# The seven-product down projection: activation forms made in steps between products, and T4 by a negation on ScalarE and an accumulating DMA

## The chip, the core and the metric

The kernel runs on one core of a Trainium2 chip. The metric is the device time of one execution in microseconds. An engine is named by the profile's short names: PE (TensorE, matmuls), DVE (VectorE), ACT (ScalarE), POOL (GpSimd), SP (SyncE, which here only issues DMAs).

## What is computed

One layer of a decoder trunk on 256 tokens of width 2048, in float32. The mixers come first; the part that matters is the second half of the layer, with 8192 hidden columns:

```python
x = layer_norm(ALPHA * x + jnp.einsum('bse,ed->bsd', mixed, w_out[l]), ln1_g[l], ln1_b[l])
h = jnp.square(jax.nn.relu(jnp.einsum('bsd,df->bsf', x, w_up[l])))
x = layer_norm(ALPHA * x + jnp.einsum('bsf,fd->bsd', h, w_down[l]), ln2_g[l], ln2_b[l])
```

## The kernel before, in words

Every float32 operand of a matmul is split into a high part (a cast to fp32r on ACT, L90) and a low part (a subtraction on DVE, L91, `split_to`); a product is then three matmuls (hi hi, hi lo, lo hi). Weights are split in halves of 1024 columns into the tiles `hi` and `lo`, four buffers each, so the splits run up to four halves ahead of PE.

The hidden columns are cut into eight groups of 1024 (`FG`). While the down projection of group g runs, the up projection of group g+1 is made in eight units ("U": `up`, `unit_t`, 16 x 2 matmuls over one 1 MB load `raw`, then `act_up` with a copy on ACT, an addition on DVE and two activations on ACT). The activations of a group lie in `hs[g % 2]`.

The down projection of groups 0 to 6 runs by seven products in place of eight (Winograd's form of Strassen's scheme). Blocks of activations: A11, A12 (first 128 tokens), A21, A22 (last 128 tokens), each by the first and second 512 hidden columns of the group. Their forms are S1 = A21 + A22, S2 = S1 - A11, S3 = A11 - A21, S4 = A12 - S2. The eight forms, split, lie in `forms` (the tile `ms`). Weights come in blocks b11, b12, b21, b22 of 1 MB (`load_blocks`, one buffer each; b12 lies in `ry`); DVE makes from them T1 = b12 - b11 (L902), T2 = b22 - T1 (L905), T3 = T2 - b11 (L910), T4 = b21 - T2 (L913). A "pair" p is one half of the 2048 output columns: pair a is p = 0, pair b is p = 1. `pair_steps` yields between its products, which come in the order 1 (A11 b11), 2 (A12 b21), 3 (S4 b22), 6 (S2 T2), 5 (S1 T1), 7 (S3 T3), 4 (A22 T4). In the seventh group (g = 6) only pair a runs by seven products; its other half is made by `plain` ("c" and "d"), with A11 to A22 as they are.

Results of a product either stay in PSUM (`pk`; products 1, 5, 6, 7 of pair a) or are copied by ACT to a tile `new` (four buffers, shared with the sums of the forms) and added in SBUF by an accumulating DMA that POOL issues (L891), into `acc` (tile `rx`) or `macc` (tile `ry`). `pair_sums(1)`, in the last of these groups, and `pair_sums(0)`, after them, add the kept products up on DVE.

The order of the stage is written out by hand, a letter a step:

```python
TURNS = "UUaaaUaaaUaUbbbUbbbUbU"
LAST = "UUUaaaUaUaUaUaUcd"
...
if n == 0:
    make_blocks(g)
elif n == 1:
    make_sums(g)
elif n == 3 and g == FG - 2:
    pair_sums(1)
```

So splits of the blocks are written behind the first step of a group and the sums with their splits behind the second. From this text a scheduler of the framework fixes the order on each engine and each DMA queue ahead of the run: what it holds to be ready goes first, earlier text before later. Each engine then works strictly in its order. All loads of weights go through SP's queue.

Of the kernel before, what the change touches and what calls it, by code (L numbers as in the profile page):

```python
# [11 lines left out]
F32 = mybir.dt.float32  # L12
F32R = mybir.dt.float32r
AF = mybir.ActivationFunctionType
ALU = mybir.AluOpType
PSUM = bass.MemoryType.PSUM

P = 128
# [6 lines left out]
FG = 8  # L25
# [23 lines left out]
def trunk_kernel(ctx: ExitStack, tc: tile.TileContext, xT, x, w_qi, w_t, w_va, w_vm0, w_vm, w_vc,  # L49
                 w_oam, w_oc, w_up4, w_up, w_down, w_dnl, conv, bif, gm, gc, lamv, g1, b1, g2, b2, out):  # L50
    nc = tc.nc
# [37 lines left out]
    def split_to(src, hi, lo, eng=nc.vector):  # L89
        nc.scalar.copy(hi, src)  # L90
        eng.tensor_sub(lo, src, hi.bitcast(F32))  # L91
# [3 lines left out]
    def split(raw, a, b, eng=nc.vector):  # L95
        pool = wpools[turn[0] % len(wpools)]
        turn[0] += 1
        hi = pool.tile([P, 1024], F32R, tag="hi", name="hi", bufs=4)
        lo = pool.tile([P, 1024], F32R, tag="lo", name="lo", bufs=4)
        split_to(raw[:, a:b], hi[:, :b - a], lo[:, :b - a], eng)  # L100
        return hi, lo
# [121 lines left out]
    def mx(name):  # L223
        return psm.tile([P, 512], F32, tag="mx", name=name)
# [115 lines left out]
    def qk():  # L340
        return [tp.tile([P, S], F32, tag=n, name=n, bufs=2) for n in ("qh", "kh")]

    for h in range(HA):
        q, k = qk()
# [73 lines left out]
    for c in range(4):  # L418
        n = VM_N[c]
        src = [w_vm0[g] for g in range(4)] if c == 0 else [w_vm[c - 1, g] for g in range(4)]  # L420
# [93 lines left out]
    for h in range(HM):  # L514
        q, k = qk()
# [97 lines left out]
    for h in range(HC):  # L613
        q, k = qk()
# [7 lines left out]
    for c in range(4):  # L622
        pss = run_units([w_oam[c, g] for g in range(3)], 512, ms, range(12))
        for t in range(2):
            a = acc[:, t, 512 * c:512 * c + 512]
# [185 lines left out]
    def up(g, m):  # L811
        h = hs[g % 2]
        unit_t(w_up[FT * g + m - 4], lambda ps: act_up(ps, h, m))
# [7 lines left out]
    A11, A12, A21, A22, S1, S2, S3, S4 = range(8)  # L821
    HT = FT // 2
    forms = ms.rearrange("p a b -> p (a b)").rearrange("p (f s k t) -> p f s k t", f=8, s=2, k=HT)
# [5 lines left out]
    def blocks_of(h):  # L829
        return [[h[:, HT * k:HT * k + HT, P * t:P * t + P] for k in range(2)] for t in range(2)]  # L830

    def make_blocks(g):
        h = hs[g % 2]
        for t in range(2):
            src = h[:, :, P * t:P * t + P].rearrange("p (f k) t -> p f k t", f=2)
            split_to(src, forms[:, 2 * t:2 * t + 2, 0], forms[:, 2 * t:2 * t + 2, 1])

    def make_sums(g):
        a = blocks_of(hs[g % 2])

        def form(f, op, x, y):
            d = fp.tile([P, HT, P], F32, tag="new", name="sum", bufs=4)
            op(d, x, y)
            split_to(d, forms[:, f, 0], forms[:, f, 1])
            return d

        s1 = form(S1, nc.vector.tensor_add, a[1][0], a[1][1])
        s2 = form(S2, nc.vector.tensor_sub, s1, a[0][0])
        form(S3, nc.vector.tensor_sub, a[0][0], a[1][0])
        form(S4, nc.vector.tensor_sub, a[0][1], s2)  # L850

    def load_blocks(g, p):
        b11, b22, b21 = (fp.tile([P, 2048], F32, tag=n, name=n, bufs=1) for n in ("b11", "b22", "b21"))
        b12 = ry[:, 2048:4096]
        nc.sync.dma_start(b11, w_down[g, 2 * p, 0])
        nc.sync.dma_start(b12, w_down[g, 2 * p + 1, 0])
        nc.sync.dma_start(b22, w_down[g, 2 * p + 1, 1])
        nc.sync.dma_start(b21, w_down[g, 2 * p, 1])
        return b11, b12, b22, b21

    def product(g, p, i, f, b):

        if p == 0 and i in KEPT:
            if g == 0:
                kept[i] = mx("pk")
            ps, first, last = kept[i], g == 0, g == FG - 2
        else:
            ps, first, last = psb.tile([P, 512], F32, tag="big", name="pp"), True, True
        for q in range(2):
            hi, lo = split(b, 1024 * q, 1024 * q + 1024)  # L870
            for kk in range(2):
                k = 2 * q + kk
                w_hi, w_lo = hi[:, 512 * kk:512 * kk + 512], lo[:, 512 * kk:512 * kk + 512]
                nc.tensor.matmul(ps, forms[:, f, 0, k, :], w_hi, start=first and k == 0, stop=False)  # L874
                nc.tensor.matmul(ps, forms[:, f, 0, k, :], w_lo, start=False, stop=False)  # L875
                nc.tensor.matmul(ps, forms[:, f, 1, k, :], w_hi, start=False, stop=last and k == HT - 1)  # L876
        if p == 0 and i in KEPT:
            return
        if i in KEPT:
            a = macc[:, KEPT[i]]  # L880
            if g == 0:
                nc.scalar.copy(a, ps)
                return
        else:
            a = out_block(p, *((0, 0), (0, 1), (1, 0))[i - 2])
            if g == 0:
                nc.vector.scalar_tensor_tensor(a, a, ALPHA, ps, ALU.mult, ALU.add)
                return
        d = fp.tile([P, 512], F32, tag="new", name="new", bufs=4)
        nc.scalar.copy(d, ps)  # L890
        nc.gpsimd.dma_start(a, d, accum_op=ALU.add)  # L891

    def out_block(p, t, c):
        return acc[:, t, 1024 * p + 512 * c:1024 * p + 512 * c + 512]

    def pair_steps(g, p, blocks):

        b11, b12, b22, b21 = blocks
        product(g, p, 1, A11, b11)
        yield  # L900
        product(g, p, 2, A12, b21)
        nc.vector.tensor_sub(b12, b12, b11)  # L902
        yield
        product(g, p, 3, S4, b22)
        nc.vector.tensor_sub(b22, b22, b12)  # L905
        yield
        product(g, p, 6, S2, b22)
        yield
        product(g, p, 5, S1, b12)
        nc.vector.tensor_sub(b11, b22, b11)  # L910
        yield
        product(g, p, 7, S3, b11)
        nc.vector.tensor_sub(b21, b21, b22)  # L913
        yield
        product(g, p, 4, A22, b21)
        if p == 0 and g < FG - 2:
            pairs["b"] = pair_steps(g, 1, load_blocks(g, 1))
        yield
# [20 lines left out]
    def plain(g, c):  # L939

        pss = [psb.tile([P, 512], F32, tag="big", name="pst") for _ in range(2)]
        for i in range(2):
            raw = load_raw(w_down[g, c, i], 2048)
            for hf in range(2):
                hi, lo = split(raw, 1024 * hf, 1024 * hf + 1024)
                for kk in range(2):
                    k = 2 * hf + kk
                    w_hi, w_lo = hi[:, 512 * kk:512 * kk + 512], lo[:, 512 * kk:512 * kk + 512]
                    for t in range(2):
                        f = 2 * t + i  # L950
                        first, last = (i, k) == (0, 0), (i, k) == (1, HT - 1)
                        nc.tensor.matmul(pss[t], forms[:, f, 0, k, :], w_hi, start=first, stop=False)  # L952
                        nc.tensor.matmul(pss[t], forms[:, f, 0, k, :], w_lo, start=False, stop=False)  # L953
                        nc.tensor.matmul(pss[t], forms[:, f, 1, k, :], w_hi, start=False, stop=last)  # L954
        for t in range(2):
            a = acc[:, t, 512 * c:512 * c + 512]
            nc.vector.tensor_add(a, a, pss[t])
# [13 lines left out]
    fp = ctx.enter_context(tc.tile_pool(name="fp", bufs=1))  # L971
# [1 line left out]
    hs[1] = fp.tile([P, FT, S], F32, name="h1")  # L973


    TURNS = "UUaaaUaaaUaUbbbUbbbUbU"
    LAST = "UUUaaaUaUaUaUaUcd"
    for g in range(FG - 1):
        pairs = {"a": pair_steps(g, 0, load_blocks(g, 0))}
        units = iter(range(FT))  # L980
        for n, what in enumerate(TURNS if g < FG - 2 else LAST):
            if what == "U":
                up(g + 1, next(units))
            elif what in "cd":
                plain(g, "cd".index(what) + 2)
            else:
                next(pairs[what])
            if n == 0:
                make_blocks(g)
            elif n == 1:  # L990
                make_sums(g)
            elif n == 3 and g == FG - 2:
                pair_sums(1)
    pair_sums(0)

# [87 lines left out]
```

## Time and profile before

| | us |
|---|---|
| runs, median (lowest to highest) of 3 | 1206.28 (1202.72 to 1206.58) |
| the profiled execution | 1202.33 |
| its span | 1200.3 |
| PE busy in the span | 1151.7 |
| DVE busy | 939.6 |
| ACT busy | 699.8 |
| POOL busy | 65.7 |

The down-projection stage with its up-projection units lies at about 520 to 1130 us; groups 0 to 5 begin every 88 to 91 us. In the timelines of the profile an instruction's row gives its start, its duration and, in brackets, how long its engine had stood idle and what released it. Durations of neighbours on one engine overlap by some 0.1 us.

### The profile page before, as it was taken

How to read it: one execution, taken by the hardware profiler on the slowest of the kernel's cores; microseconds unless marked ns; L12 is line 12 of the kernel's file. 1: busy time of each engine (PE TensorE's matmuls, PEld its weight loads, DVE VectorE, ACT ScalarE, POOL GpSimd, SP SyncE). 2: the span in 40 equal slices, each digit the busy share in tenths (PEclk: the TensorE clock that was granted, in tenths of full speed). 3: DMA queues.
4: the chain of work that ended last, by engine and by line, in shares of the span. 5: the costliest groups of instructions: out<-in, count | busy, mean ns of one | idle time of the engine just before them, and what ended most of it. 6: DMA issues, size and time to landing. Idle time of an engine off the chain costs nothing. (4 is left out here: it accounts for less than half of the span.)

```text
span 1200.3 us, 15706 instructions
## 1 busy us (share of the span) xinstructions
PE 1151.7 (96%) x5960; PEld 981.9 (82%) x5960; DVE 939.6 (78%) x1225; ACT 699.8 (58%) x1010; POOL 65.7 (5%) x87
## 2 busy tenths in 40 slices
PE   9999999999999999989999999999989999989996
PEld 7998899988888887878787877878878878768885
DVE  5596556677667589598998898898898898878757
ACT  5444446545555453566676676676676676656641
POOL 1000000000000010000000100101101101100002
PEclk9999999999999999999999999999999999989998
DMA  8654446644854582545546847847837947844561
GB/s 303 217 186 165 144 159 235 212 172 175 300 187 147 179 305 100 185 166 220 210 158 229 273 147 236 278 136 237 289 123 236 293 119 237 264 166 132 175 246 70
DMA packets 42566, 240.41 MB, mean 200 GB/s; under 512 B 4982, under 2 KB 5372, under 8 KB 18556
## 3 DMA queue, kind: packets, MB, share of 16 engines
q1 hardware_dynamic: 33564, 218.19, 50.5%
q0 software_dynamic: 8208, 18.09, 7.7%
q10 hardware_dynamic: 720, 3.15, 0.7%
q8 instruction: 46, 0.75, 0.3%
q14 instruction: 28, 0.23, 0.1%
HBM read 223.41 MB, written 2.11 MB: 188 GB/s over the span
## 5 line engine op out<-in xcount | busy, mean ns | idle before, releaser
L158 PE MATMUL ps<-xs,hi 128*128 128x512 f32 x1488 | 526.4, 394 | 0.0
L90 ACT CAST hi<-raw 128x1024 fp32r<-128x1024 f32 (+4 forms) x307 | 310.5, 1015 | 288.0 <-PE ps L158 106.2
L91 DVE TENSOR_TENSOR lo<-raw,hi 128x1024 fp32r<-128x1024 f32 (+4 forms) x305 | 358.6, 1187 | 149.0 <-ACT hi L90 147.6
L159 PE MATMUL ps<-xs,lo 128*128 128x256 f32 x1488 | 421.8, 283 | 12.7 <-DVE lo L91 12.4
L158 PEld LDWEIGHTS ps<-xs,hi 128*128 128x128 f32 x1488 | 280.6, 189 | 58.7 <-issue 0.3
L159 PEld LDWEIGHTS ps<-xs,lo 128*128 128x128 f32 x1488 | 282.3, 190 | 19.6 <-DVE lo L91 18.3
L91 DVE TENSOR_TENSOR lo<-b,hi 128x1024 fp32r<-128x1024 f32 x156 | 185.6, 1221 | 32.1 <-ACT hi L90 32.1
L90 ACT CAST hi<-b 128x1024 fp32r<-128x1024 f32 x156 | 160.9, 1048 | 47.2 <-PE ps L158 15.9
L874 PE MATMUL pp<-hi,ms 128*128 128x512 f32 x252 | 101.4, 402 | 17.0 <-ACT hi L90 16.9
L875 PE MATMUL pp<-lo,ms 128*128 128x512 f32 x252 | 100.5, 399 | 0.4 <-DVE lo L91 0.3
L876 PE MATMUL pp<-hi,ms 128*128 128x512 f32 x252 | 100.3, 398 | 0.0
L208 PE MATMUL pst<-hi,xs 128*128 128x384 f32 (+3 forms) x224 | 79.0, 353 | 0.0
L209 PE MATMUL pst<-lo,xs 128*128 128x384 f32 (+3 forms) x224 | 77.7, 347 | 0.0
L210 PE MATMUL pst<-hi,xs 128*128 128x384 f32 (+3 forms) x224 | 77.6, 346 | 0.0
L874 PEld LDWEIGHTS pp<-hi,ms 128*128 128x128 f32 x252 | 47.7, 189 | 33.2 <-ACT hi L90 22.3
L875 PEld LDWEIGHTS pp<-lo,ms 128*128 128x128 f32 x252 | 47.6, 189 | 12.1 <-DVE lo L91 1.3
L876 PEld LDWEIGHTS pp<-hi,ms 128*128 128x128 f32 x252 | 47.8, 190 | 10.8
L891 POOL DMA_DIRECT2D rx<-new x33 | 28.1, 852 | 496.0 <-ACT new L890 441.0
L875 PE MATMUL pk<-lo,ms 128*128 128x512 f32 x112 | 44.4, 397 | 1.6 <-DVE lo L91 1.6
L874 PE MATMUL pk<-hi,ms 128*128 128x512 f32 x112 | 43.7, 398 | 1.5 <-ACT hi L90 1.5
L876 PE MATMUL pk<-hi,ms 128*128 128x512 f32 x112 | 44.4, 396 | 0.0
L890 ACT COPY new<-pp 128x512 f32<-128x512 f32 x53 | 30.9, 584 | 22.5 <-PE pp L876 22.5
(290 smaller groups left out, 1530.9 us busy)
## 6 DMA issues: line engine op xcount, KB each, us to landing
raw<-in_w_up_dram SPq DMA_DIRECT2D x64, 1024.0 KB, 7.2
b<-in_w_down_dram SPq DMA_DIRECT2D x39, 1024.0 KB, 6.8
raw<-in_w_t_dram SPq DMA_DIRECT2D x33, 1024.0 KB, 4.8
ry<-in_w_down_dram SPq DMA_DIRECT2D x13, 1024.0 KB, 5.1
raw<-in_w_oam_dram SPq DMA_DIRECT2D x12, 1024.0 KB, 4.9
raw<-in_w_vm_dram SPq DMA_DIRECT2D x12, 768.0 KB, 4.2
rx<-new POOLq DMA_DIRECT2D x33, 256.0 KB, 3.6
raw<-in_w_dnl_dram SPq DMA_DIRECT2D x8, 1024.0 KB, 7.1
```

Of the source, the lines that this page charges most:

```text
L90: nc.scalar.copy(hi, src)
L91: eng.tensor_sub(lo, src, hi.bitcast(F32))
L158: nc.tensor.matmul(ps, hi[:, P * kk:P * kk + P], xs[:, k, :], start=(k == 0), stop=False)
L159: nc.tensor.matmul(ps[:, 0:S], lo[:, P * kk:P * kk + P], xs[:, k, 0:S], start=False, stop=(k == KT - 1))
L208: nc.tensor.matmul(pss[t][:, :n], a_hi, w_hi, start=first, stop=False)
L209: nc.tensor.matmul(pss[t][:, :n], a_hi, w_lo, start=False, stop=False)
L210: nc.tensor.matmul(pss[t][:, :n], a_lo, w_hi, start=False, stop=last)
L874: nc.tensor.matmul(ps, forms[:, f, 0, k, :], w_hi, start=first and k == 0, stop=False)
L875: nc.tensor.matmul(ps, forms[:, f, 0, k, :], w_lo, start=False, stop=False)
L876: nc.tensor.matmul(ps, forms[:, f, 1, k, :], w_hi, start=False, stop=last and k == HT - 1)
L890: nc.scalar.copy(d, ps)
L891: nc.gpsimd.dma_start(a, d, accum_op=ALU.add)
```

## The change

- The forms come in steps. After the first step of a group the splits of A11 and A12 and the sums S1 and S2; after the second the sum S4 and the splits of S4 and S2; after the fourth the split of S1, S3 with its split, and A22 (in the seventh group A21 and A22). A21 is not split any more in the other groups, where no product reads it.
- T4 is not subtracted on DVE any more. After product 5 and T3, ACT multiplies b22 (which holds T2) by -1 in place, and a DMA issued by POOL adds b21 to it, read from DRAM a second time. Product 4 reads b22. So b21's tile is free after product 2, and b22's only after product 4.
- The turns change: in groups 0 to 5 "aaaUaaaUaU" becomes "aaaUaaUaUa" for either pair, in the seventh group a U moves ahead of product 7 and product 4 comes between "c" and "d". `pair_sums(1)` comes one step later.

```diff
--- before.py
+++ after.py
@@ -829,25 +829,25 @@
     def blocks_of(h):
         return [[h[:, HT * k:HT * k + HT, P * t:P * t + P] for k in range(2)] for t in range(2)]
 
-    def make_blocks(g):
+    def make_blocks(g, t):
         h = hs[g % 2]
-        for t in range(2):
-            src = h[:, :, P * t:P * t + P].rearrange("p (f k) t -> p f k t", f=2)
+        src = h[:, :, P * t:P * t + P].rearrange("p (f k) t -> p f k t", f=2)
+        if t == 0 or g == FG - 2:
             split_to(src, forms[:, 2 * t:2 * t + 2, 0], forms[:, 2 * t:2 * t + 2, 1])
-
-    def make_sums(g):
+        else:
+            split_to(src[:, 1], forms[:, A22, 0], forms[:, A22, 1])
+
+    sums = {}
+
+    def make_form(g, f):
         a = blocks_of(hs[g % 2])
-
-        def form(f, op, x, y):
-            d = fp.tile([P, HT, P], F32, tag="new", name="sum", bufs=4)
-            op(d, x, y)
-            split_to(d, forms[:, f, 0], forms[:, f, 1])
-            return d
-
-        s1 = form(S1, nc.vector.tensor_add, a[1][0], a[1][1])
-        s2 = form(S2, nc.vector.tensor_sub, s1, a[0][0])
-        form(S3, nc.vector.tensor_sub, a[0][0], a[1][0])
-        form(S4, nc.vector.tensor_sub, a[0][1], s2)
+        op, x, y = {S1: (nc.vector.tensor_add, a[1][0], a[1][1]), S2: (nc.vector.tensor_sub, sums.get(S1), a[0][0]),
+                    S3: (nc.vector.tensor_sub, a[0][0], a[1][0]), S4: (nc.vector.tensor_sub, a[0][1], sums.get(S2))}[f]
+        sums[f] = fp.tile([P, HT, P], F32, tag="new", name="sum", bufs=4)
+        op(sums[f], x, y)
+
+    def split_form(f):
+        split_to(sums[f], forms[:, f, 0], forms[:, f, 1])
 
     def load_blocks(g, p):
         b11, b22, b21 = (fp.tile([P, 2048], F32, tag=n, name=n, bufs=1) for n in ("b11", "b22", "b21"))
@@ -908,11 +908,13 @@
         yield
         product(g, p, 5, S1, b12)
         nc.vector.tensor_sub(b11, b22, b11)
+
+        nc.scalar.mul(b22, b22, -1.0)
+        nc.gpsimd.dma_start(b22, w_down[g, 2 * p, 1], accum_op=ALU.add)
         yield
         product(g, p, 7, S3, b11)
-        nc.vector.tensor_sub(b21, b21, b22)
         yield
-        product(g, p, 4, A22, b21)
+        product(g, p, 4, A22, b22)
         if p == 0 and g < FG - 2:
             pairs["b"] = pair_steps(g, 1, load_blocks(g, 1))
         yield
@@ -973,8 +975,8 @@
     hs[1] = fp.tile([P, FT, S], F32, name="h1")
 
 
-    TURNS = "UUaaaUaaaUaUbbbUbbbUbU"
-    LAST = "UUUaaaUaUaUaUaUcd"
+    TURNS = "UUaaaUaaUaUabbbUbbUbUb"
+    LAST = "UUUaaaUaUaUUaUcad"
     for g in range(FG - 1):
         pairs = {"a": pair_steps(g, 0, load_blocks(g, 0))}
         units = iter(range(FT))
@@ -986,10 +988,19 @@
             else:
                 next(pairs[what])
             if n == 0:
-                make_blocks(g)
+                make_blocks(g, 0)
+                make_form(g, S1)
+                make_form(g, S2)
             elif n == 1:
-                make_sums(g)
-            elif n == 3 and g == FG - 2:
+                make_form(g, S4)
+                split_form(S4)
+                split_form(S2)
+            elif n == 3:
+                split_form(S1)
+                make_form(g, S3)
+                split_form(S3)
+                make_blocks(g, 1)
+            if n == 4 and g == FG - 2:
                 pair_sums(1)
     pair_sums(0)
```

## Rows read from the trace of the kernel before

**Rows 1.** The page, part 1: busy us (share of the span) xinstructions, whole span

```profile
PE 1151.7 (96%) x5960; PEld 981.9 (82%) x5960; DVE 939.6 (78%) x1225; ACT 699.8 (58%) x1010; POOL 65.7 (5%) x87
```

**Rows 2.** Windows; columns PE, PEld, DVE, ACT, POOL, clock, DMA, GB/s

```profile
701.00:790.00 89.00, 84.62 (x426) 70.46 (x425) 78.34 (x71) 61.31 (x85) 8.51 (x10) 1.00 0.68 219
```

**Rows 3.** Timeline of PE: start us, us, engine, line, operation, [idle before <-releaser]

```profile
711.89 0.39 PE L158 MATMUL ps<-xs,hi 128*128 128x512 f32 x1
717.44 0.63 PE L874 MATMUL pk<-hi,ms 128*128 128x512 f32 x2
725.84 0.40 PE L158 MATMUL ps<-xs,hi 128*128 128x512 f32 x1
```

**Rows 4.** PE's waits (total us, times, longest): 520:612, 612:1040, 1040:1062

```profile
PE pk L875 <- DVE lo L91: 1.6, 1, 1.6
PE pk L874 <- ACT hi L90: 1.5, 1, 1.5
PE pp L874 <- ACT hi L90: 1.4, 1, 1.4
...
PE pp L874 <- ACT hi L90: 15.6, 10, 3.1
PE ps L159 <- DVE lo L91: 4.8, 8, 0.7
...
PE ps L159 <- DVE lo L91: 7.6, 2, 5.7
```

**Rows 5.** Timeline of PE, two waits of the group from 701 us

```profile
705.26 0.50 PE L874 MATMUL pp<-hi,ms 128*128 128x512 f32 x1 [2.24 <-ACT hi L90]
727.23 0.50 PE L874 MATMUL pp<-hi,ms 128*128 128x512 f32 x1 [0.98 <-ACT hi L90]
```

**Rows 6.** Windows of busy time, two stretches with a lowered clock

```profile
960.00:980.00 20.00, 17.86 (x83) 14.71 (x82) 18.25 (x22) 15.12 (x23) 0.55 (x1) 0.91 0.28 104
1060.00:1080.00 20.00, 18.86 (x86) 15.88 (x87) 19.53 (x23) 16.33 (x25) 0.56 (x1) 0.84 0.45 158
```

**Rows 7.** Groups by line, DVE, 701:790: xcount | busy us, mean ns | idle before

```profile
L91 DVE TENSOR_TENSOR lo<-b,hi 128x1024 fp32r<-128x1024 f32 x24 | 28.5, 1220 | 5.5 <-ACT hi L90 5.5
L913 DVE TENSOR_TENSOR b<-b,b 128x2048 f32<-128x2048 f32 x2 | 4.6, 2286 | 0.0
L843 DVE TENSOR_TENSOR sum<-h 128x512 f32<-128x512 f32 x3 | 2.1, 684 | 0.0
L91 DVE TENSOR_TENSOR ms<-sum,ms 128x512 fp32r<-128x512 f32 x4 | 2.6, 683 | 0.0
L91 DVE TENSOR_TENSOR ms<-h,ms 128x1024 fp32r<-128x1024 f32 x2 | 2.4, 1214 | 0.0
```

**Rows 8.** Timeline of ACT, the casts of product 4 in pair a

```profile
726.13 2.00 ACT L90 CAST hi<-b 128x1024 fp32r<-128x1024 f32 x2 [1.59 <-DVE b L913]
```

**Rows 9.** Groups by line, 540:1150, ACT's largest cast

```profile
L90 ACT CAST xs<-h 128x2048 fp32r<-128x2048 f32 x1 | 1.9, 1926 | 0.0
```

**Rows 10.** Instructions on tile new: duration ns min/median/max, and landing times

```profile
L891 POOL DMA_DIRECT2D rx<-new x33: 836/849/905, 621.7 to 1118.0; - x33
DMA to landing us min/median/max: 3.2/7.2/10.8
```

**Rows 11.** The page, part 3: packets, MB, share of 16 engines

```profile
q1 hardware_dynamic: 33564, 218.19, 50.5%
q0 software_dynamic: 8208, 18.09, 7.7%
```

**Rows 12.** Timeline of ACT, casts at the end of pair b

```profile
778.99 2.00 ACT L90 CAST hi<-raw 128x1024 fp32r<-128x1024 f32 x2 [2.98 <-DMA raw<-in_w_up_dram]
```

**Rows 13.** The page, part 6: DMA issues xcount, KB each, us to landing

```profile
b<-in_w_down_dram SPq DMA_DIRECT2D x39, 1024.0 KB, 6.8
```

**Rows 14.** Timeline of DVE at the entry of the last group

```profile
1043.39 0.69 DVE L931 TENSOR_TENSOR ry<-ry 128x512 f32<-128x512 f32 x1 [4.78 <-DMA ry<-new]
1056.12 0.69 DVE L936 TENSOR_TENSOR rx<-rx,ry 128x512 f32<-128x512 f32 x1 [5.90 <-DMA rx<-new]
```

## What the change will do to the time

> **What bounds the kernel now.** I read the busy shares first: TensorE (PE) is busy for 1151.7 of 1200.3 us [rows 1]. The matmuls are the same before and after, so the change can only win what PE loses in the down-projection stage and its surroundings, about 520 to 1062 us. Second, the windows of that stage: in one group (701 to 790 us) PE is busy 84.62 of 89.00 us, DVE 78.34, ACT 61.31, and the DMA engines 0.68 [rows 2]. PE is the bound and DVE is close behind, so a burst of DVE work shows as a hole on PE. Third, the smallest time of a group: a unit of the up projection ("U") lasts 717.44 - 711.89 = 5.55 us, three products last 725.84 - 717.44 = 8.40, or 2.80 each [rows 3]. Eight U and 14 products make 44.4 + 39.2 = 83.6 us, against 89: some 5 us of each group are not matmul.
>
> Fourth, PE's waits, in three stretches [rows 4]: 520 to 612 us (first group) three of 1.6, 1.5 and 1.4 us beside a small one; 612 to 1040 (five groups) 15.6 us in ten waits for ACT's casts and 4.8 in eight for DVE's subtractions; 1040 to 1062 (entry of the last group) 7.6 us in two. Together 32.5. Two places make the ten waits: one per group ahead of the first products, as at 705.26 (2.24 us), and one per group where product 4 of pair a begins, as at 727.23 (0.98 us) [rows 5]. Five of the second kind at 0.98 are 4.9 us, which leaves 15.6 - 4.9 = 10.7 for the first. To this comes the clock: in 960 to 980 us PE is granted 0.91 of the higher level (2.4 GHz) and in 1060 to 1080 us 0.84 [rows 6], stretches at 1.2 GHz after PE had stood still. A share of 0.09 and 0.16 of 20 us is 1.8 + 3.2 = 5.0 us. The ceiling of the gain is so 32.5 + 5.0 = 37.5 us.
>
> **The change, part by part.**
>
> *Forms in steps.* Before, all forms of a group are made after its first two U: four sums at 0.684 us, four splits of a sum at 0.683, two splits of blocks at 1.214 on DVE [rows 7], in all 2.74 + 2.73 + 2.43 = 7.9 us, and DVE runs them ahead of product 1's own subtractions (1.22 each). After, three sums, two splits and one block split come there (2.05 + 1.37 + 1.21 = 4.6 us), the rest behind the second product: one sum and three splits of 512 columns, A22 alone among them (2.7 us; A21 is not split any more in six of the seven groups, 0.5 us less each). So 3.3 us leave the place whose waits are 1.04 to 3.07 us. I take all of the 10.7 us as gone, and of the first group's 1.6. What is late next: between product 1 and product 3 DVE has 2.44 per product and the 2.7 us of forms, 10.0 us in all for three products, where PE needs 8.4 us: 1.6 us late if DVE has no lead, nothing if it has. Bounds 0 to 1.6 us in each of seven groups, 0 to 11; I take 3, since the DVE comes there 3.3 us earlier than now.
>
> *T4 without DVE.* Thirteen subtractions of 2.286 us (L913) leave DVE [rows 7], 4.6 us per group. They stand on the path in two ways: ACT's cast of product 4 waits for them (1.59 us before the cast at 726.13 [rows 8]), which is the 0.98 us wait of PE in each pair a, 4.9 us; and in pair b they delay the subtractions of the next U, the 4.8 us in eight waits. I take 4.9 and 4.0.
>
> In its place ACT multiplies 128x2048 by -1. No such instruction is in the trace; the nearest row is ACT's cast of 128x2048, 1.93 us [rows 9]; between that and two casts of half the size (2.1 us) I take 1.9, 13 of them, 3.8 us per group on an engine that has 27 us free of 89 [rows 2]. It waits for T3's subtraction (which reads b22) and for product 6's splits, and ACT's casts for products 5 and 7 queue behind it. PE has up to two products or two U split ahead, 5.6 to 11 us, so the 1.9 us is covered; without the cover it would cost 1.9 x 13 = 25.
>
> The accumulating DMA of 1 MB: GpSimd (POOL) issues it, and the nearest row of an issue is 0.85 us [rows 10]; POOL is idle 80 of 89 us [rows 2], and behind the issue wait only the accumulations of results. Its work: queue q1 moved 218.19 MB in 50.5% of the span, 2.78 us per MB; q0 moved 18.09 MB in 7.7%, 92.4 us [rows 11]. Four plain loads of 1.05 MB among q0's take 11.7 at q1's rate, so the 53 accumulations of 13.9 MB took 80.7, or 5.8 us per MB. T4's 1.05 MB is 6.1 us of all engines, 12 per group on top of 0.68 x 89 = 60: 72 of 83.6 us. Its landing: an accumulation of 256 KB lands after 3.2 us at least, 7.2 median, 10.8 at most [rows 10]. Lower end 3.2 + three quarters of 6.1 = 7.8; upper end four such at the median, 28.8. I take 7.8 + (7.2 - 3.2) = 12, by the lower end and the queueing that the median row shows. The Trainium skill ("DMA: Bandwidth & Descriptors", "Anatomy of one DMA — SWDGE (gpsimd) path") fits 2.0 us and bytes over 436 GB/s, an estimate of 4.4 us for 1 MB; for 256 KB it gives 2.6 where the row has 7.2, so the measurement decides against it; by it the sum would stay 26 and the first rival below would fall away.
>
> The cover: product 6 starts on PE at 717.44 [rows 3], where b22's last reads end; the negation and the issue take until about 721.5; products 6 and 5, U, product 7, U keep PE until 717.44 + 8.4 + 11.1 = 736.9, and product 4's own cast and subtraction need 2.3 before that. So T4 has 734.6 - 721.5 = 13 us. A landing of 12 costs nothing, with 1 us to spare.
>
> *Loads and the order of turns.* b21 is free after product 2 and b22 only after product 4, the reverse of now. Now SP issues the load of b21 last, behind product 4's splits, and weights of U queue behind it there; ACT waits 2.98 us for such weights ahead of 778.99 [rows 12], just before the forms of the next group. After, b21's load moves far ahead, and b22 is needed one product later than b21 was. From pair a to b the U between is gone: b22, free when product 4 is split, has the U ahead of product 4 and products 4, 1 and 2 (5.55 + 8.4 = 14 us, less 2.3 for product 3's splits) against 6.8 us of a load [rows 13]: covered. I count no gain for it; it is a reserve for the 3 us above. More evenly set U add no matmul.
>
> *Entry of the last group.* DVE stands 4.78 us at 1043.39 and 5.90 us at 1056.12 for accumulations to land [rows 14], while the next U waits behind. That is 7.6 us of PE and 3.2 of clock. The sums now come one step (a product, 2.8 us) later, and there is no load of b21 beside them; but the last product of pair b also comes one U later. Between 0 and 10.8 I take 6.
>
> *Sum.* 10.7 + 1.6 + 4.9 + 4.0 + 6 + 1.8 (the clock after 972, whose wait goes) = 29.0, less 3 = 26. The profiled execution, 1202.3 us (span 1200.3 and 2.0 around it), becomes 1176; the median of the runs shown lies 4 us higher, 1206.3, and becomes 1180.
>
> **The rivals.**
>
> *T4 lands late (the other side).* Decides from 13 us between issue and landing. Each us beyond holds ACT's cast of product 4, all casts behind it, and PE, in 13 pairs: at 17 us it is 4 x 13 = 52 us lost against 26 won, 1206 + 26 = 1232; at 16 about 1219. For it: the median row of 7.2 us for a quarter of the bytes, and 72 of 83.6 us of DMA work. Against: b21's load has left this stretch by then (it is free after product 2), and b11's and b22's come only after products 7 and 4. The skill (same page, "Queues, rings and completion order") says that each engine takes turns between the queues packet by packet, so T4 could not be starved by the loads but would share with them; no row here shows packets. 0.12.
>
> *The stalls only move.* DVE falls from 78 to 73 us of a group, but three products in a row still ask 10.0 us in 8.4; the late forms cost 1.6 us in seven groups (11) and the last group gains nothing (6 less): 26 - 8 - 6 = 12 won, 1194; with POOL or ACT some us late as well, 1202. For it: the holes sit at bursts, not at the mean. Against: PE's waits are no longer than 3.1 us except at the last group, less than the DVE time that leaves their places. 0.20.
>
> *All holes close.* The last group's too: 37.5, so 1169. 0.13.
>
> **How the numbers follow.** Forecast 1180 with its neighbourhood (1172 to 1190): 0.55. All holes close 0.13, stalls move 0.20, T4 late 0.12. The range from 1167 to 1203 holds the first three except the worst of the second, about 0.83. 0.3% (3.6 us) is what a measurement of this kernel can tell from no change: faster has 0.55 + 0.13 + 0.12 of the stalls' case, 0.80; same 0.09, of the stalls' case and a T4 a little late; slower 0.11.
>
> **What would show it.** Right: no wait of PE above 1 us ahead of product 1 or at product 4, DVE some 73 us a group, groups of 84 to 86 us; the DMA into b22 landing in less than 13 us; no clock below 1.00 before 1040. Wrong: a wait of ACT's cast for the DMA into b22 in every pair; PE waiting inside product 3 behind the forms; a wait of DVE for the accumulations at the last group as long as now.

## The result: slower by 1.3%

The changed kernel takes 1222.06 us (median; 1217.25 to 1223.14) where the kernel before takes 1205.8 beside it: a ratio of 1.0132, 95% interval [1.01, 1.0164]. The forecast was 1180 with a range of 1167 to 1203; the sign was wrong. The profiled execution took 1222.28 us, its span 1220.2.

The page of the changed kernel: busy times (answers [rows 1]), two DMA queues with their share of 16 engines ([rows 11]), and DMA issues with KB and us to landing ([rows 13]).

```profile
PE 1166.0 (96%) x5960; PEld 988.5 (81%) x5960; DVE 910.0 (75%) x1212; ACT 714.1 (59%) x1023; POOL 77.5 (6%) x100
...
q1 hardware_dynamic: 33564, 218.19, 50.0%
q0 software_dynamic: 10080, 31.72, 13.1%
...
b<-in_w_down_dram SPq DMA_DIRECT2D x39, 1024.0 KB, 6.7
b<-in_w_down_dram POOLq DMA_DIRECT2D x13, 1024.0 KB, 12.3
```

DVE lost its 30 us, as meant, and ACT is busy 14 us more. But PE is busy 14 us more too, for the same 5960 matmuls: some of them ran at the lower clock. T4's DMA lands after 12.3 us; the prediction had 12.

Windows of the changed kernel (columns as in [rows 2]): one group's length, then two stretches of 20 us behind the ends of groups ([rows 6]).

```profile
723.00:816.00 93.00, 86.56 (x417) 71.21 (x416) 72.83 (x68) 62.70 (x86) 10.22 (x12) 0.96 0.76 229
780.00:800.00 20.00, 15.89 (x73) 13.32 (x72) 14.91 (x16) 12.63 (x21) 1.70 (x2) 0.83 0.91 299
...
1060.00:1080.00 20.00, 13.69 (x64) 11.33 (x63) 12.54 (x13) 8.85 (x15) 1.57 (x2) 0.83 0.81 248
```

DVE is down from 78 to 73 us of a group, but a group grew from 89 to 93 us or more, and the DMA engines work 0.76 of it (0.91 around its end).

What PE, DVE and ACT waited for in the whole stage, 520 to 1090 us of the changed kernel (total us, times, longest); PE's rows answer [rows 4].

```profile
PE pp L875 <- DVE lo L91: 28.8, 24, 4.1
PE ps L159 <- DVE lo L91: 8.9, 6, 6.3
PE pk L874 <- ACT hi L90: 1.5, 1, 1.5
PE pp L874 <- ACT hi L90: 1.0, 2, 0.5
...
DVE ry L902 <- DMA b<-in_w_down_dram: 16.4, 5, 4.5
DVE ry L932 <- DMA ry<-new: 9.6, 1, 9.6
...
ACT hi L90 <- DMA b<-in_w_down_dram: 42.3, 17, 5.5
```

The ten waits for ACT's casts (15.6 us) are all but gone. In their place PE waits for DVE's low parts, and ACT and DVE wait for loads. PE's waits came to 32.5 us in three stretches before, 32.7 with a small one; now to 40.2: 7.5 more. The records show PE's clock at 0.5 of the higher level in six stretches of this stage, each at the end of a stall of 3 us or more: 34.1 us in all, where before it was 10.2 in two. Half of the difference, some 12 us, is lost. 7.5 + 12 is the 20 us that the span grew.

One of the stalls in full: timelines of the changed kernel's engines, 764 to 795 us (start, duration, engine, line, operation, idle time and what ended it).

```profile
764.46 1.92 ACT L912 ACTIVATE b<-b 128x2048 f32<-128x2048 f32 x1 [0.28 <-DVE lo L91]
...
766.68 0.85 POOL L913 DMA_DIRECT2D b<-in_w_down_dram  x1 [7.51 <-ACT half L808]
...
773.21 0.33 SPq L855 DMA_DIRECT2D b<-in_w_down_dram  x1
...
779.09 1.05 ACT L90 CAST hi<-b 128x1024 fp32r<-128x1024 f32 x1 [2.53 <-DMA b<-in_w_down_dram]
...
780.17 1.23 DVE L91 TENSOR_TENSOR lo<-b,hi 128x1024 fp32r<-128x1024 f32 x1 [2.29 <-ACT hi L90]
785.93 2.29 DVE L902 TENSOR_TENSOR ry<-ry,b 128x2048 f32<-128x2048 f32 x1 [4.54 <-DMA b<-in_w_down_dram]
788.14 1.22 DVE L91 TENSOR_TENSOR lo<-b,hi 128x1024 fp32r<-128x1024 f32 x1
...
789.42 0.80 PE L875 MATMUL pp<-lo,ms 128*128 128x512 f32 x1 [4.11 <-DVE lo L91]
790.44 0.63 PE L874 MATMUL pp<-hi,ms 128*128 128x512 f32 x1
```

The negation starts at 764.46 and T4's DMA is issued at 766.68; ACT's cast for product 4 has to wait 2.53 us for it, until 779.09. PE doesn't stand for that: product 4's first matmuls begin at 783.5. In the middle of that transfer, at 773.21, SP issues the next pair's b11 (L855), which lands only 12.6 us later. T1 (L902), which needs b11, stands in DVE's order between the two low parts of product 4: DVE waits 4.54 us for the load, the second low part follows at 788.14, and PE, in product 4, has stood for 4.11 us. After that its matmuls have 0.63 us instead of 0.4.

b11's load, all thirteen, in the changed kernel (times to landing: least, median, most):

```profile
L855 SPq DMA_DIRECT2D b<-in_w_down_dram x13: 328/328/328, 511.2 to 1057.0; - x13
...
DMA to landing us min/median/max: 6.0/11.2/12.6
```

In the kernel before the same line shows 5.8, 6.8 and 8.9. Of ACT's 42.3 us of waits for tiles b, 36.5 are for T4's DMA (ten waits in 13 pairs), 4.8 for b11 and 1.0 for b22's reload.

### The profile page after: what moved, and what is told of

It reads as the page before. It is cut to its first block, busy times and chain, and to the rows that moved or that the text cites. A ratio compares the mean times of both kernels' runs of the same rounds, so it can differ in the third digit from the quotient of the medians.

```text
span 1220.2 us, 15761 instructions
## 1 busy us (share of the span) xinstructions
PE 1166.0 (96%) x5960; PEld 988.5 (81%) x5960; DVE 910.0 (75%) x1212; ACT 714.1 (59%) x1023; POOL 77.5 (6%) x100
## 3 DMA queue, kind: packets, MB, share of 16 engines
q0 software_dynamic: 10080, 31.72, 13.1%
## 4 chain that ended last, share of the span: by engine, by line
PE 71%; DVE 9%; DMA 9%; issue 7%; ACT 5%; SPq 0%; DVEq 0%; POOL 0%; ACTq 0%
PE ps L158 22%; PE ps L159 12%; DMA b<-in_w_down_dram 7%; DVE lo L91 6%; PE pst L208 5%; PE pst L209 5%; PE pst L210 5%; ACT hi L90 2%; PE psl L657 2%; PE psl L655 2%; PE psl L658 2%; PE pk L876 1%; PE pk L875 1%; DVE b L905 1%; DMA ry<-new 1%
## 5 line engine op out<-in xcount | busy, mean ns | idle before, releaser
L159 PEld LDWEIGHTS ps<-xs,lo 128*128 128x128 f32 x1488 | 285.0, 192 | 17.2 <-DVE lo L91 15.2
L90 ACT CAST hi<-b 128x1024 fp32r<-128x1024 f32 x156 | 160.2, 1048 | 83.1 <-DMA b<-in_w_down_dram 42.3
L875 PE MATMUL pp<-lo,ms 128*128 128x512 f32 x252 | 104.9, 416 | 28.8 <-DVE lo L91 28.8
L874 PEld LDWEIGHTS pp<-hi,ms 128*128 128x128 f32 x252 | 48.0, 191 | 13.1 <-ACT hi L90 1.7
L808 ACT ACTIVATE half<-half 128x256 f32<-128x256 f32 x60 | 24.8, 413 | 49.4 <-DVE half L807 48.6
## 6 DMA issues: line engine op xcount, KB each, us to landing
b<-in_w_down_dram POOLq DMA_DIRECT2D x13, 1024.0 KB, 12.3
```

The lines of the kernel that those rows point to most:

```text
L159: nc.tensor.matmul(ps[:, 0:S], lo[:, P * kk:P * kk + P], xs[:, k, 0:S], start=False, stop=(k == KT - 1))
L808: nc.scalar.activation(half, half, AF.Relu)
```

## The experiments

Three theories of what T4's DMA costs. A: its 1 MB slows other loads, b11's above all, and DVE stands for it at T1. B: product 4 waits for T4's own landing. C: the chain costs, whatever the bytes: negation, issue, wait, late release of b22. Ratios are to the kernel before on the same chip.

### Each part alone

**Forms and turns, T4 as before.**

```diff
-        nc.scalar.mul(b22, b22, -1.0)
-        nc.gpsimd.dma_start(b22, w_down[g, 2 * p, 1], accum_op=ALU.add)
         yield
         product(g, p, 7, S3, b11)
+        nc.vector.tensor_sub(b21, b21, b22)
         yield
-        product(g, p, 4, A22, b22)
+        product(g, p, 4, A22, b21)
```

> The changed kernel with T4 back on DVE (b21 minus T2, product 4 on b21); forms in steps and new turns stay. Theory A (T4's accumulating DMA fills the DMA engines, the next pair's b11 lands late, 12.6 us instead of 6.8, and DVE stands at T1's subtraction, L902, ahead of product 4's second subtraction): the waits of DVE for b11 fall from 16.4 us to 10 or less, PE's waits in the stage from 40 to under 25 us, the time to 1180 to 1195. Rival B (product 4 waits for T4's own landing, 12.3 us): the same fall. Rival C (the turns without a U between product 4 and what follows): still 1205 to 1222. Rival D (the forms in steps): still 1206 or more, with PE waiting ahead of product 3.

1178.0 us, ratio 0.9793 [0.9772, 0.9813]. The rest of the change is worth 25 us; T4's part takes 44 from it. One thing came out otherwise than expected: DVE's wait for b11 at T1 hardly fell. PE and DVE, 520 to 1090 us of this kernel, and the landings of b11 (L855):

```profile
PE pp L875 <- DVE lo L91: 4.2, 6, 1.4
...
DVE ry L902 <- DMA b<-in_w_down_dram: 14.4, 5, 4.1
...
DMA to landing us min/median/max: 6.2/7.9/10.3
```

T1 stands between the low parts of product 4 here too, at the ends of four groups, and DVE waits nearly as long, but PE stalls behind it 1.4 us at most. In the changed kernel DVE is ready for T1 later (at 781.39, 8.2 us behind b11's issue, where here it is some 6 us behind), because product 4's cast has waited for T4. So b11 lands 3 us later (11.2 against 7.9), DVE's own wait is hardly longer, and yet PE stalls. How long DVE waits at T1 is no measure of the cost.

**T4 alone**, in the kernel before (the edit above the other way round, with the old forms and turns):

> The kernel before with only T4 changed (negation on ACT, accumulating DMA); forms and turns as before, so only one U stands between product 5 and product 4. Theory A: 1212 to 1230, DVE waiting 12 us or more in all for b11 at T1. Rival B: with a U (5.55 us) less ahead of product 4, every pair waits some 5 us for T4: 13 x 5 on top, 1260 to 1290. Rival C: at or under before, 1190 to 1206.

1248.59 us, ratio 1.0381 [1.036, 1.0403]. PE and ACT, 520 to 1090 us of this kernel:

```profile
PE pp L874 <- ACT hi L90: 33.0, 18, 3.1
...
ACT hi L90 <- DMA b<-in_w_down_dram: 84.1, 11, 8.3
```

In the old turns products 6, 5 and 7 stand in a row, so T4 has one U of 5.55 us less to land in than the 13 us that I worked out: some 7.5 us, with landings of 11.9. That is B as the rival in the prediction had it: (11.9 - 7.5) x 13 = 57 by its price, 46 measured. The time lies between what I had for A and for B; DVE has no wait for b11 here, so A's road doesn't show in it.

**The change with the old turns:**

```diff
-    TURNS = "UUaaaUaaUaUabbbUbbUbUb"
-    LAST = "UUUaaaUaUaUUaUcad"
+    TURNS = "UUaaaUaaaUaUbbbUbbbUbU"
+    LAST = "UUUaaaUaUaUaUaUcd"
```

> The changed kernel with the old turns (forms in steps and the new T4 stay). Theory A: 1205 to 1230. Rival B: 1260 to 1290, PE waiting at product 4 behind ACT's cast for the DMA into b22. Rival C: under 1200.

1256.81 us, ratio 1.0446 [1.0427, 1.0465]; ACT waits up to 9.0 us for T4. So forms in steps save nothing where T4 sets the pace.

**Forms alone** (forms in steps, old turns, T4 on DVE) and **turns alone** (the kernel before with the two strings of the new turns):

> The kernel before with the forms in steps alone (old turns, T4 on DVE). The prediction's terms: the wait ahead of the first products goes (12 us and the slow clock behind it) and 3 us come back behind product 2: 1188 to 1196. If the turns carry the gain of forms and turns together (25 us): 1198 to 1206.

> The kernel before with the new order of turns alone (forms made at once after the second U, T4 a subtraction on DVE). Forms alone gave 1198.5, forms and turns 1178. If the two add up, turns alone are worth 15 to 20 us: 1185 to 1190. If the turns need the forms in steps (three products follow the first U, so a late form stalls all three), 1195 to 1210, with PE's waits ahead of product 1 as now (2.2 us in six groups).

Forms alone: 1198.54 us, ratio 0.9943 [0.9917, 0.997]. Turns alone: 1177.75 us, ratio 0.9768 [0.9736, 0.98], the same as forms and turns together. The two don't add up: the turns have the whole gain. PE's waits in 612 to 1040 us, the five groups of [rows 4], of forms alone first:

```profile
PE pk L874 <- ACT hi L90: 9.2, 5, 2.0
PE ps L159 <- DVE lo L91: 5.0, 13, 0.7
```

and of turns alone:

```profile
PE pk L875 <- DVE lo L91: 3.5, 5, 0.8
PE pp L875 <- DVE lo L91: 2.4, 4, 1.4
```

With the forms in steps PE still waits 1.8 us per group in the first products; with the turns and all forms made at once, 0.7. One thing that changes there is the order of loads. SP's timeline at the end of a group, kernel before:

```profile
767.83 0.33 SPq L858 DMA_DIRECT2D b<-in_w_down_dram  x1
768.25 14.55 SPq L86 DMA_DIRECT2D raw<-in_w_up_dram  x4
```

and with the new turns alone:

```profile
765.65 0.33 SPq L86 DMA_DIRECT2D raw<-in_w_up_dram  x1
773.56 0.33 SPq L858 DMA_DIRECT2D b<-in_w_down_dram  x1
```

Before, weights of U (L86) are issued behind b21's load (L858), and ACT waits 2.98 us for them just ahead of the forms [rows 12], 11.4 us over the stage. With the new turns one of them goes 8 us ahead of that load, and no wait of ACT for such weights is left among its waits. That this order is the whole gain of the turns was not tried by itself.

### Which part of T4

**The negation alone.** Forms and turns, with ACT's negation, and T4 a DVE addition of b21:

```diff
         nc.scalar.mul(b22, b22, -1.0)
-        nc.gpsimd.dma_start(b22, w_down[g, 2 * p, 1], accum_op=ALU.add)
         yield
         product(g, p, 7, S3, b11)
+        nc.vector.tensor_add(b21, b21, b22)
         yield
-        product(g, p, 4, A22, b22)
+        product(g, p, 4, A22, b21)
```

> Forms in steps, new turns, T4 on DVE as b21 plus the negated T2: ACT's 13 negations of 1.92 us are added and no DMA. Theories A and B: the negation is covered, 1176 to 1184. If ACT's queue behind the negation is what costs: 1195 to 1205 (13 x 1.9 = 25 on top of 1178).

1181.25 us, ratio 0.9815 [0.9796, 0.9833]: some 3 us more than forms and turns, so nearly covered, as priced.

**The chain without the bytes**, and **half of the bytes:**

```diff
-        nc.gpsimd.dma_start(b22, w_down[g, 2 * p, 1], accum_op=ALU.add)
+        nc.gpsimd.dma_start(b22[:, :16], w_down[g, 2 * p, 1][:, :16], accum_op=ALU.add)
```

(`:1024` in place of `:16` for half)

> The changed kernel with the accumulating DMA cut to the first 16 of 2048 columns, so T4 lacks b21's rest: negation, issue by POOL, a short landing, product 4 on b22 and b22's late release stay, the traffic goes. Theory A and rival B (a transfer that takes 12 us): 1170 to 1185. Rival C (b22 is free only after product 4, so its load comes late): 1205 or more.

> The kernel after, but T4's accumulating DMA adds only the first 1024 of 2048 columns (0.5 MB in place of 1 MB; the rest of T4 is then only -T2, so this part of the computation is left out). Order, engines and waits stay. With 8 KB in its place the time was 1174.6 us (the chain alone), with 1 MB 1222. If the cost is a slope in bytes (each byte takes the loads' share), 1195 to 1202, half way. If it is a threshold (a cover of some 13 us that the landing passes or doesn't, and 12.6 us for b11 that DVE's order passes or doesn't), half the bytes land in some 8 us, b11 in 8 to 9 us, and the time is 1175 to 1186, no wait of ACT for the DMA into b22, and at most 7 us at 1.2 GHz.

With 8 KB: 1174.64 us, ratio 0.9756 [0.9732, 0.978]. C falls: negation, issue, wait and b22's late release cost nothing together. With 512 KB: 1192.32 us, ratio 0.9893 [0.9862, 0.9924]. So 0, 18 and 47 us for 8, 512 and 1024 KB: neither a threshold nor quite a slope, since the second half costs 1.7 times the first. T4 lands after 5.2, 8.5 and 12.3 us, b11 after 5.6, 8.7 and 11.2. DVE's wait at T1 is 28.1 us in twelve with 512 KB, more than with 1 MB, which again is not the cost.

**T1 out of DVE's way.** T1 issued behind the low parts of product 2, so that it no longer stands among those of product 4:

```diff
         product(g, p, 2, A12, b21)
-        nc.vector.tensor_sub(b12, b12, b11)
+        traced = nc.cur_bb.bb.instructions
+        last = next(i for i in reversed(traced) if i.engine == mybir.EngineType.DVE)
+        with tc.issue_after(last):
+            nc.vector.tensor_sub(b12, b12, b11)
```

> The changed kernel with T1's subtraction (b12 minus b11) issued on DVE only behind product 2's own subtractions, as the source has it, instead of ahead of the last pair's product 4; the transfers stay. Theory A: the waits of 3 to 4 us at the end of five groups (17 us) and the slow clock behind them (12 us more than before) go: 1188 to 1200, b11 still landing after 10 us or more. Rivals B and C: 1215 to 1225, as the changed kernel, since T4's landing and the turns are the same. Rival D: 1215 or more, more DVE work standing ahead of product 3.

1223.68 us, ratio 1.017 [1.015, 1.0191]: no gain. DVE's wait for b11 is gone, but T1 now runs in the busiest stretch, T2 behind it comes late, and PE waits 17.2 us in six waits for product 6's casts. By the expectation this time speaks for B, C or D and against A; but the edit moved the cost to another place, so it doesn't tell A from B.

**b11 out of T4's way.** b11 and b21 take turns in two buffers, so b11's load starts once product 2 has freed b21's tile:

```diff
-        b11, b22, b21 = (fp.tile([P, 2048], F32, tag=n, name=n, bufs=1) for n in ("b11", "b22", "b21"))
+        b11, b21 = (fp.tile([P, 2048], F32, tag="b11_21", name=n, bufs=2) for n in ("b11", "b21"))
+        b22 = fp.tile([P, 2048], F32, tag="b22", name="b22", bufs=1)
```

> The kernel after, T4 by the accumulating DMA with all its bytes, but b11 and b21 take turns in two buffers, so that the next pair's b11 is loaded into the tile that product 2 frees and no longer waits for product 7; T1's subtraction on DVE then has no load to wait for, while b21's load takes b11's late place. If the stalls come from T1 standing in DVE's order for a late b11: the wait of DVE at T1 goes (16 us in 5 of them) and PE's stalls at the ends of groups with it, 1185 to 1205. If product 4's wait for T4's landing is enough by itself: 1212 to 1225, ACT's wait for b22's DMA as long as now (42 us in 17). If b21's later load now holds T2 or product 2: above 1222, DVE waiting for b21 at product 2.

1196.5 us, ratio 0.9927 [0.9902, 0.9953]. b11 lands after 4.9 us (median), T1 waits for b12's load instead (12.1 us in nine waits, none over 2.5), and all of the lower clock in 600 to 1040 us is gone. So 26 of the 44 us come from b11 landing late where DVE's order has T1, as A says. The kernel changes two things at once, though: with b11 early the order on DVE also has T1 behind both low parts of product 4:

```profile
760.73 2.36 DVE L91 TENSOR_TENSOR lo<-b,hi 128x1024 fp32r<-128x1024 f32 x2
...
765.18 2.29 DVE L903 TENSOR_TENSOR ry<-ry,b 128x2048 f32<-128x2048 f32 x1 [2.09 <-DMA ry<-in_w_down_dram]
```

How much of the 26 us each of the two brings was not tried. b21's load now runs beside T4 (11.1 us), and nobody waits for it. 18 us stay. In this kernel they are seen at T4 itself and at b22; timelines of POOL, ACT, SP, ACT and PE, 718 to 744 us of this kernel (its lines are one higher):

```profile
718.91 0.86 POOL L914 DMA_DIRECT2D b<-in_w_down_dram  x1 [8.51 <-ACT half L808]
...
731.10 1.05 ACT L90 CAST hi<-b 128x1024 fp32r<-128x1024 f32 x1 [4.44 <-PE ps L159]
...
734.69 0.33 SPq L858 DMA_DIRECT2D b<-in_w_down_dram  x1
...
741.66 1.05 ACT L90 CAST hi<-b 128x1024 fp32r<-128x1024 f32 x1 [2.08 <-DMA b<-in_w_down_dram]
...
742.76 0.50 PE L875 MATMUL pp<-hi,ms 128*128 128x512 f32 x1 [0.44 <-ACT hi L90]
744.02 0.50 PE L876 MATMUL pp<-lo,ms 128*128 128x512 f32 x1 [0.76 <-DVE lo L91]
```

ACT stands 4.44 us ahead of product 4's cast, 12.2 us behind T4's issue (the row names PE, which had long been done; T4's landing fits). b22 is so released late, its next load is issued at 734.69 and lands at 741.66, and PE waits for it in the next pair's product 3. ACT waits 28.1 us for T4 and 10.0 for b22's reload in this kernel.

**The same bytes in two halves, and early b11 without the bytes.** In the kernel with early b11:

```diff
-        nc.gpsimd.dma_start(b22, w_down[g, 2 * p, 1], accum_op=ALU.add)
+        for q in range(2):
+            cols = slice(1024 * q, 1024 * q + 1024)
+            nc.gpsimd.dma_start(b22[:, cols], w_down[g, 2 * p, 1][:, cols], accum_op=ALU.add)
```

> The kernel with early b11 (1196.5 us), and T4's accumulating DMA issued as two of 1024 columns each. Bytes and traffic are the same; ACT's first cast of product 4 needs only the first half, which lands some 8 us after its issue in place of 12. If what is left is T4's landing ahead of product 4 (4.4 us of ACT in pair a) and b22's reload behind it, 1184 to 1192. If it is the traffic on the other loads or the shared buffers, 1194 to 1200.

> The kernel with early b11 (1196.5 us), but the accumulating DMA adds only 16 of 2048 columns, so T4 lacks the rest of b21 (left out of the computation). Buffers, order and waits stay. If the 18 us that early b11 leaves are the bytes of T4's DMA, by its landing or by b22's reload, 1172 to 1180. If the shared buffers (b21's load late, b11's moved) cost something by themselves, 1185 to 1196.

Two halves: 1208.31 us, ratio 1.0037 [1.0015, 1.006], 12 us more, against my expectation. The landings of these 26 DMAs:

```profile
L916 POOL DMA_DIRECT2D b<-in_w_down_dram x26: 846/1042/1292, 544.6 to 1099.4; - x26
...
DMA to landing us min/median/max: 8.0/10.1/17.7
```

The first half does come sooner (8.0 us at best), but the second later than the whole did: up to 17.7 us, where the whole needed 12.7 at most. ACT's waits for loads into b tiles rise from 38.1 to 54.5 us, those for T4 from 28.1 to 50.2, while those for b22's reload fall from 10.0 to 4.3. A later landing of T4 goes with more time, which fits B, if by a road I hadn't meant. Without the bytes: 1178.73 us, ratio 0.9781 [0.9747, 0.9815]. So the shared buffers cost no more than 4 us, and the 18 us hang on T4's bytes.

**The traffic alone.** T4 on DVE, and two plain 1 MB writes to DRAM in place of T4's DMA. In the first try they read b22:

```diff
+        for copy in copies:
+            nc.gpsimd.dma_start(copy, b22)
```

> The changed kernel with T4 on DVE again (b21 plus the negated T2), ACT's negation kept, and in place of the accumulating DMA two plain DMAs by POOL of the negated T2 to DRAM, 1 MB each, that nothing waits for but the next load of b22: the traffic (some 5.6 us of all engines per pair, by q1's 2.78 us per MB) without product 4's wait. Theory A (the traffic makes the next loads late): 1200 to 1225, b11 landing after 10 us or more and DVE waiting over 20 us for it at T1. Rival B (product 4 waits for T4's transfer): 1175 to 1190, as without the DMA (1178).

1241.63 us, ratio 1.0313 [1.0289, 1.0337], but b22's reload waited for the copies (97 us on SP's queue), so this tells nothing about traffic. In the second they read a tile that is never rewritten, and nothing waits for them:

```diff
+        nc.gpsimd.dma_start(tick16, b22[:, :16])
+        last = nc.cur_bb.bb.instructions[-1]
+        with tc.issue_after(last):
+            for copy in copies:
+                nc.gpsimd.dma_start(copy, acc_src)
```

> Forms and turns, T4 on DVE from a negated T2 (1181 us), and at the place of T4's DMA, issued by GpSimd, two plain 1 MB writes of a resident tile to DRAM that nothing waits for (2 MB of 2.78 us per MB, 5.6 us of all engines, near the 5.0 to 5.8 of the accumulating one). If T4's cost is what its traffic does to the loads of the weights: b11 lands after 10 to 13 us in place of 8, DVE waits for it at T1, 1195 to 1215. If it is only that product 4 waits for T4's own landing: 1178 to 1186. If accumulating hurts more than plain bytes do, b11 lands after 8 to 9 us and the time is 1182 to 1190.

1255.74 us, ratio 1.0424 [1.0394, 1.0455]: 74 us more than the negation alone, much more than expected. PE, DVE and ACT in 520 to 1090 us of this kernel:

```profile
PE ps L159 <- DVE lo L91: 34.6, 12, 7.1
...
DVE ry L905 <- DMA b<-in_w_down_dram: 74.9, 12, 9.1
...
ACT hi L90 <- DMA b<-in_w_down_dram: 41.6, 7, 7.8
```

b11 lands after 11.9 us (15.9 at most) where it took 8.0, and DVE waits for it at T1 (L905 here) in twelve of thirteen pairs. T1 stands behind both low parts of product 4 here, and PE stalls behind it all the same, in the U that follows. Traffic that no instruction waits for costs more than T4 does, by A's road. Why 2 MB of plain writes weigh so much more than 1 MB accumulated stays open.

## Why the prediction was wrong

**T4's cover: the step that failed.** The landing was right (12 forecast, 12.3 measured), in part by luck: the median of 7.2 us for 256 KB that it was built on mixes accumulations into `rx` and `ry`, whose medians were 3.6 and 8.6. Its work was about right too (q0's share gives 13.1% of 1220.2 us less 92.4, 67 us for 13.6 MB, or 4.9 us per MB; I had 5.8). The error is "A landing of 12 costs nothing, with 1 us to spare". I compared the landing with product 4's start on PE alone, and that much held: PE's waits for ACT's casts fell to 2.5 us in the whole stage. But I asked nothing of what else lies in these 12 us. b11's load is issued inside T4's transfer (773.21 between 766.68 and 779.09), though the text held it to be out of the way, since b11's and b22's loads "come only after products 7 and 4". The DMA engines are 0.92 busy from 766 to 786 us, b11 lands after 11.2 us in place of 6.8 (7.9 with the same turns and no such DMA), and T1 waits for it on DVE ahead of product 4's second low part. An early b11, with T1 in another place, brings 26 of the 44 us back.

The other 18 hang on T4's bytes as well, but their road stays open. In the kernel with early b11, ACT waits for T4's landing and for b22's reload, which the text called "covered" with a load of 6.8 us and a landing on time; in the changed kernel itself ACT waits for that reload once, 1.0 us. The Trainium skill ("DMA: Bandwidth & Descriptors", "Anatomy of one DMA — SWDGE (gpsimd) path") gives an estimate of 4.4 us for this megabyte; the landings of 5.2 us for 8 KB and 12.3 for 1 MB decide against it here, beside other loads.

**The rival "T4 lands late"** named the right transfer, and its 1219 for a landing of 16 us is near the 1222 measured, but by luck: the landing was 12.3 us, 13.2 at most, and PE's stalls are behind b11.

**The clock** was counted as a gain of 1.8 us. The new stalls of 3 to 6 us bring six stretches at 1.2 GHz: some 12 us lost, more than the waits themselves grew.

**Forms ahead of product 1** (10.7 and 1.6 us): right in the sum, wrong in the cause. Forms alone left 9.2 of the 10.7. The waits go with the turns, with all forms still in one block. Splits behind ACT's 2.98 us wait for U's weights [rows 12] were the hint; I saw it and wrote "I count no gain for it". The 3 us for late forms never showed: forms and turns together take what turns alone take.

**T4 off DVE** (4.9 and 4.0): not needed for it. The wait of PE at product 4 [rows 5] and the waits for DVE's subtractions [rows 4] are gone with the turns alone, with T4 still on DVE.

**Entry of the last group** (6 us): the turns bring it, since DVE's wait for accumulations falls from 4.78 and 5.90 us [rows 14] to 0.5 with turns alone. With T4's DMA on the same queue they land later (17.3 us at most, 10.8 before), DVE waits 9.6 us, and PE 6.3: about as long as before.

**So the sum.** 26 us was a good size for what is here to win: 26 to 28 with turns alone (by the medians and by the ratio), 25 with forms. That is luck in part, since most of its terms are won by the turns, for which I counted nothing. The part I priced at nothing lost 44.

**The marks named in advance.** DVE's 73 us of a group and a landing below 13 us came true and were no proof. Groups of 84 to 86 us, no wait of PE above 1 us at product 4, and no lowered clock before 1040 us, did not. Of the marks against, ACT's wait for the DMA into b22 came ten times in 13 pairs, and DVE's wait for the accumulations at the last group stayed (9.6 us).

The version to keep is the kernel before with the new turns alone, 1177.75 us: two strings of the change.

## What to carry to other kernels

- A transfer has two prices: its own landing against its user, and what it does to each load issued while it runs. List those loads from the DMA queue's timeline, add the stretched landing to each, and look where on an in-order engine its user stands and what is queued behind.
- A landing in time for its own user is not yet free: here the cover of 13 us held for PE, and the change lost all the same. Ask what the change is worth without that part, and what it costs one step late.
- Reordering steps may win all that a rewrite of their work promises, so price the order by itself first: which loads move ahead of which.

## What the runs showed of the hardware

- An accumulating DMA from DRAM into SBUF, issued by POOL beside other loads, landed after 5.2 us for 8 KB, 8.5 for 512 KB and 12.3 for 1 MB: some 7 us per MB on top of 5. Its work is 4.9 us of all 16 engines per MB against 2.78 for a plain load [rows 11].
- Two accumulating DMAs of 512 KB, issued one behind the other, end later (up to 17.7 us) than one of 1 MB (up to 12.7).
- A 1 MB load that starts within such a transfer of 1 MB takes 10 to 13 us (b21's 9.9 to 12.2 with early b11), in place of 5 to 8 (the same load with 8 KB in the transfer's place).
